# The last group of a layer's opening: all eight pairs turned by transfers, each asked for one visit behind its plane copy, and 16 conditioning passes moved behind the group

## The chip, the cores and the metric

The kernel runs on one core of one Trainium2 chip, as one program. The metric is the device time of one execution in microseconds (us); less is better. Engines are named as in the profile: PE is TensorE (PEld its weight loads), DVE is VectorE, ACT is ScalarE, POOL is GpSimd, SP is SyncE. SP computes nothing here: it holds the queue that issues nearly all transfers, in the order in which they are written.

## The reference

One conditioned decoder layer over 256 tokens of width 2048, in float32:

```python
mod = (c_act @ w_ada[l] + b_ada[l]).reshape(b, N_MOD, D_MODEL)
h = modulate(rms_norm(x, norm_ffn1[l]), mod[:, 0], mod[:, 1])
x = x + 0.5 * mod[:, 2][:, None, :] * swiglu(h, w_ffn1_gu[l], w_ffn1_down[l])
h = modulate(rms_norm(x, norm_mix[l]), mod[:, 3], mod[:, 4])
x = x + mod[:, 5][:, None, :] * token_mixing(h, w_in[l], ...)
...
def swiglu(h, w_gu, w_down):
    gate, up = jnp.split(h @ w_gu, 2, axis=-1)
    return (jax.nn.silu(gate) * up) @ w_down
```

What matters here is the first `swiglu` (the gate and up products have 5632 columns each) and the nine conditioning vectors `mod`, each a product of one row with a 2048 x 2048 block of `w_ada`.

## The kernel before

**Products.** A weight of 512 columns arrives in tiles of 128 x 4 x 512 floats (1 MB, pool `raws` with four buffers, line 106). Two of its four blocks at a time are split into a high and a low part: ACT casts the high part (`wh`, line 375), DVE subtracts it (`wl`, line 377). Pool `wsp` (line 107) holds three such pairs, so ACT can cast at most three pairs ahead of PE. For each pair PE runs 12 matmuls of 128x512 (`products`, line 354): high by high, low by high, high by low, over two halves of the tokens.

**The opening.** Because the normed input becomes ready only slowly, the first 16 chunks (8 pairs of a gate chunk and an up chunk) are not computed one after the other over the whole depth, but in four groups of blocks of the depth: blocks 0-1, 2-5, 6-11 and 12-15. Each group goes over all 16 chunks in `visit` (line 1193). The last group, `final`, has four blocks, so a visit loads one tile of 1 MB and has two pairs of weights, 24 matmuls. At the end of each turn of the loop (line 1245) `ready` asks for the tile of the next visit and casts its first pair; then `turn_step` (line 326) lets every transfer in hand do one step. After each odd visit a pair of chunks is complete and `swiglu_up` (line 695) forms silu(gate) x up for two halves of the tokens.

**Turning the result.** The product that follows needs that result transposed, in one of two ways. By PE: four transposes of 128x128 into PSUM and one eviction for each half (`transpose_to`, lines 518 and 519). By transfer (`turn_by_dma`, line 525), in three steps for each half: `apart`, two ACT copies that separate the 16-bit planes (line 535, tile `flat`); `turn`, a transposing transfer that SP issues (line 540) from `flat` into a tile `back`; `together`, two ACT copies from `back` into place (line 551). ACT's plane copies are told to stand behind the last cast issued so far. The pool `back` has four buffers (line 112): a fifth `turn` takes the buffer of the first, and so waits until the first one's `together` has read it. Before the change, pairs 0 to 5 of the group are turned by transfers and pairs 6 and 7 by PE. The steps are spread over the visits by a generator, `later` (line 651).

**Conditioning.** DVE works through `w_ada` in passes of 128x512 (line 220), four to a tile of 1 MB, which SP loads at line 215. `tick` (line 318), called after each pair of weights, does as many passes as `pace["rate"]` says. In the last group of the opening it does one pass for each pair during the first eight visits (16 passes, four tiles, taken from the pool `raws`); behind the opening, in `ffn_up` and in the product that follows, the rest, (192 - 64) / 117 to a pair. The passes of this block are due before the next norm, after that product.

**What sets the order.** Only SP's order is written by hand (line 103): its transfers stand exactly as the code issues them, and each waits for its own buffers before the next is looked at. The order on the other engines is set when the program is built, within the constraints named above; it is then fixed.

Of the kernel before, what the change touches and what calls it, by code (L numbers as in the profile page):

```python
# [77 lines left out]
def layer_kernel(  # L78
# [42 lines left out]
    def nm(s):  # L121
        uid[0] += 1
        return f"{s}_{uid[0]}"
# [10 lines left out]
    def t512():  # L134
        return tmp.tile([P, CH], F32, tag="t512", name=nm("t"))
# [173 lines left out]
    pace = {"steps": iter(()), "rate": 0.0, "due": 0.0, "behind": None}  # L309
# [14 lines left out]
    turns = []  # L324
# [189 lines left out]
    def transpose_to(dest, src_of, n, ps=None):  # L514

        ps = ps or bank()
        for j in range(n):
            nc.tensor.transpose(ps[:, j * P : (j + 1) * P], src_of(j), ident)
        nc.any.tensor_copy(dest, ps[:, : n * P])
# [5 lines left out]
    def turn_by_dma(dest, src, pool=flat, tag="flat"):  # L525


        held = {}

        def apart():  # L530
            planes = pool.tile([P, CH], F32, tag=tag, name=nm("flat"))
            planes = planes.bitcast(U16).rearrange("p (i n) -> p i n", i=2)
            with tc.issue_after(cast[-1]):
                for i in range(2):
                    nc.scalar.copy(planes[:, i, :], words(src)[:, :, i])  # L535
            held["planes"] = planes

        def turn():
            turned = back.tile([P, 2, KB, P], U16, tag="back", name=nm("back"))
            nc.sync.dma_start_transpose(  # L540
                turned.rearrange("p i k n -> p (i k) n"),
                held["planes"].rearrange("p i n -> p (i n)"),
            )
            held["turned"] = turned

        into = dest.bitcast(U16).rearrange("p k (s i) -> p k s i", i=2)

        def together():
            with tc.issue_after(cast[-1]):
                for i in range(2):  # L550
                    nc.scalar.copy(into[:, :, :, i], held["turned"][:, i])  # L551

        return apart, turn, together
# [97 lines left out]
    def later(work, then=None, quick=False):  # L651

        (a0, t0, m0), (a1, t1, m1) = work
        order = [a0, a1, None, None, None, t0, t1, None, m0]
        for f in order[:7] + order[7 + quick :]:
            yield
            if f is not None:
                f()
        m1()
        if then is not None:  # L660
            then()

    def later_by_pairs(work):

        for apart, _, _ in work:
            apart()
        for _ in range(5):
            yield
        for a in range(0, len(work), 2):
            for which in (1, 2):  # L670
                yield
                for parts in work[a : a + 2]:
                    parts[which]()
# [21 lines left out]
    def swiglu_up(banks_g, banks_u, tiles, ci, parts=None, by_dma=False, behind=None):  # L695

        k0 = ci * KB
        dest = tiles[k0 // KD].rearrange("p (k s) -> p k s", s=S)
        kk = k0 % KD
        work = []  # L700
        for t in range(NT):
            s = t512()
            g, u = banks_g[t], banks_u[t]
            if parts is not None:
                nc.vector.tensor_add(s, g, parts[0][t])
                nc.vector.tensor_add(parts[1][t], u, parts[1][t])
                g, u = s, parts[1][t]
            with nullcontext() if behind is None else tc.issue_after(behind):
                nc.scalar.activation(s, g, AF.Silu)
            nc.vector.tensor_mul(s, s, u)  # L710
            if by_dma:
                work.append(turn_by_dma(dest[:, kk : kk + KB, t * P : (t + 1) * P], s))
                continue
            transpose_to(
                dest[:, kk : kk + KB, t * P : (t + 1) * P],
                lambda j: s[:, j * P : (j + 1) * P],
                KB,
            )
        if work:
            turns.append(later(work))  # L720

    def ffn_up(held, w, tiles, first, bg=None, turned=(), ahead=None):
        for ci in range(first, DFF // CH):
# [244 lines left out]
    behind = [[back.tile([P, CH], F32, tag="back", name=nm("back")) for _ in range(NT)] for _ in range(2)]  # L968
# [181 lines left out]
    groups = [range(a, b) for a, b in zip(bounds, bounds[1:])]  # L1150
# [12 lines left out]
    def begin(n, ks):  # L1163
        raw_of = [(load_blocks(n, part), part) for part in (ks[:KB], ks[KB:]) if part]
        pieces = [
            (raw[:, a : a + 2, :], part[a : a + 2])
            for raw, part in raw_of
            for a in range(0, len(part), 2)
        ]
        prepared[n] = [  # L1170
            (lambda raw=raw, part=part: split(wsp, "w", raw[:, : len(part), :], CH), part)
            for raw, part in pieces
        ]
# [19 lines left out]
    def visit(n, ks, ends, ticks=False, ends_all=False):  # L1193
        if n not in prepared:
            begin(n, ks)
        if n not in banks:
            open_banks(n, not ends_all)
        for make, part in prepared.pop(n):
            a, b = part[0] - ks[0], part[-1] + 1 - ks[0]
            hl = slice(part[0], part[-1] + 1)  # L1200
            wh, wl = make()
            products(
                banks[n],
                held.hi[:, hl, :],
                held.lo[:, hl, :],
                wh,
                wl,
                n in fresh and a == 0,
                b == len(ks) and ends,
                seeded=n in unlinted,  # L1210
            )
            if ticks:
                tick()
        fresh.discard(n)
# [18 lines left out]
    for g, ks in enumerate(groups):  # L1233
        alone.append(g == len(groups) - 2)
        del alone[:-1]
        final = g == len(groups) - 1
        if g == len(groups) - 2:
            set_pace(ROWS_FFN1, 192, place_early, 0)
        if final:
            pace["rate"], pace["ahead"] = 1.0, 1  # L1240
        order = chunks if (len(groups) - g) % 2 else chunks[::-1]
        coming = iter(()) if final else group(groups[g + 1], 1 if g == 0 else 2)
        due = 0 if final else 2 * len(groups[g + 1])
        stay = () if final else order[-2:]
        for i, n in enumerate(order):
            if g == 0 and n in firsts:
                continue
            visit(n, ks, n not in stay, g == len(groups) - 2 or final and i < 8, final or (g == len(groups) - 2 and n in stay))
            if g:
                after = [(m, ks) for m in order[i + 1 : i + 2]]  # L1250
                if not after and not final:
                    after = [(n, groups[g + 1])]
                for m, ms in after:
                    ready(m, ms)
                    if m not in banks and not final:
                        open_banks(m, not (g == len(groups) - 2 and m in stay))
            if final:
                turn_step()
            last = len(order) - 2
            if g == 0:  # L1260
                by = [min(due, -(-j * due // 12)) for j in (i - 2, i - 1)]
                by = by[1] - by[0]
            else:
                by = (i + 1) * due // last - i * due // last if i < last else i == last
            for _ in range(by + (g == 0 and i == last)):
                next(coming, None)
            if g == 0:
                for m in {2: firsts[:1], 3: (order[2], firsts[1])}.get(i, order[i - 1 : i]):
                    if m not in stay:
                        to_parts(m)  # L1270
                if i == 3:
                    columns_rest()
                if i == 5:
                    roots_in_rows()
            if n in stay or g == 0:
                continue
            if not final:
                to_parts(n)
            elif n % 2:
                swiglu_up(  # L1280
                    banks.pop(n - 1),
                    banks.pop(n),
                    tiles,
                    n // 2,
                    (part_of(n - 1), part_of(n)),
                    n // 2 < 6,
                    cast[-1],
                )
    gate = gate_row()
    tiles.append(slot())  # L1290
    row_ring.append(two_rows())
    pace["rate"] = (192 - 64) / 117
    pace["ahead"] = AQ
    ffn_up(held, gu, tiles, EARLY, turned=range(EARLY, DFF // CH))
    gate_in = gate_load(gate, 2)
# [33 lines left out]
    work = []  # L1329
# [153 lines left out]
    for ci in range(4):  # L1483
        b = in_chunk(O_SQ + ci * CH)
        work = []
# [16 lines left out]
    for a, off in ((0, O_RQ), (1, O_RK)):  # L1502
        for ci in range(2):
            b = in_chunk(off + ci * CH)
            work = []
# [93 lines left out]
    for ci in range(4):  # L1599
        b = in_chunk(O_RG + ci * CH)  # L1600
        work = []
# [11 lines left out]
    for p in range(2):  # L1613
# [8 lines left out]
        work = []  # L1622
# [146 lines left out]
```

## Time and profile before

| | us |
|---|---|
| median of 3 runs | 2367.28 (2357.96 to 2367.73) |
| the profiled execution | 2357.64 |
| its span in the profile | 2355.5 |
| PE busy in it | 2335.7 (99%) |
| DVE busy | 1673.1 (71%) |
| ACT busy | 1367.2 (58%) |
| HBM over the span | 256 GB/s |

The profile's page gives the busy time of each engine and the chain of work that ended last, followed back from the last instruction. Other views give the busy time in chosen stretches, the instructions of one engine in order of time, the waits, and for a transfer the time from its issue to its landing. In a row of the timeline the first number is the start in us from the span's start, the second the length; `SPq` is SP's queue; `<-` in square brackets names what ended an idle time.

### The profile page before, as it was taken

Reading aid. Unit: us, or ns where it says so; the run is one execution under the profiler, and the core shown is the slowest. Engines: PE = TensorE matmul, PEld = TensorE weight load, DVE = VectorE, ACT = ScalarE, POOL = GpSimd, SP = SyncE. Lnnn points to the kernel's source line nnn. Section 1 sums busy time; section 2 is a strip of 40 time slices with the busy share of each in tenths; the row PEclk is TensorE's granted clock in tenths of the full one; section 3 lists DMA queues with packets and bytes.
Section 4 is the critical chain, followed back from the end, with each engine's and each line's share of the span. In section 5 each row is a group of like instructions: output and inputs, shape, how many; then the busy total and the mean of one; then the engine's idle time right before and its main releaser. Section 6 shows DMA issues by size and latency. Waiting matters only on the chain.

```text
span 2355.5 us, 28357 instructions
## 1 busy us (share of the span) xinstructions
PE 2335.7 (99%) x10445; PEld 1918.6 (81%) x10445; DVE 1673.1 (71%) x2576; ACT 1367.2 (58%) x1888; POOL 18.3 (1%) x27
## 2 busy tenths in 40 slices
PE   8999999999999999999999999999999999999998
PEld 5888888888888888778888888888888888888887
DVE  7788888778867768976777776676555555555656
ACT  6766567455556567774556564465455454455544
POOL 0000000000000000000000000000000000000000
PEclk9999999999999999999999999999999999999999
DMA  9989889988765889876778787754767768666553
GB/s 383 375 323 361 355 294 328 336 306 293 302 237 220 293 267 255 258 212 254 267 273 306 288 310 281 272 204 179 259 237 256 242 239 268 223 231 202 193 197 125
DMA packets 191901, 630.24 MB, mean 268 GB/s; under 512 B 113105, under 2 KB 114769, under 8 KB 121233
## 3 DMA queue, kind: packets, MB, share of 16 engines
q1 hardware_dynamic: 189266, 617.41, 74.6%
q0 software_dynamic: 1600, 9.83, 1.0%
q8 instruction: 82, 1.34, 0.2%
q10 hardware_dynamic: 896, 1.19, 0.1%
q14 instruction: 57, 0.47, 0.1%
HBM read 598.47 MB, written 4.22 MB: 256 GB/s over the span
## 4 chain that ended last, share of the span: by engine, by line
PE 96%; DMA 2%; DVE 1%; ACT 1%; issue 0%; SPq 0%; DVEq 0%; ACTq 0%
PE pa L360 93%; DMA raw<-in_w_ffn_gu_dram 1%; DMA rows_x<-in_w_ada_dram 1%; PE ps L1453 0%; DVE slot L220 0%; PE pd L1369 0%; DVE wl L377 0%; ACT wh L375 0%; DMA x_sb<-in_x_dram 0%; PE ps L360 0%; PE pa L1099 0%; PE ps L895 0%; PE pd L1099 0%; DVE rows_x L220 0%; PE ps L1369 0%
## 5 line engine op out<-in xcount | busy, mean ns | idle before, releaser
L377 DVE TENSOR_TENSOR wl<-raw,wh 128x1024 fp32r<-128x1024 f32 x792 | 963.5, 1225 | 511.0 <-ACT wh L375 451.6
L375 ACT CAST wh<-raw 128x1024 fp32r<-128x1024 f32 x792 | 830.6, 1054 | 818.7 <-PE pa L360 752.6
L360 PE MATMUL pa<-wh,hh 128*128 128x512 f32 x2184 | 597.0, 391 | 3.0 <-ACT wh L375 1.7
L360 PE MATMUL pa<-wh,hl 128*128 128x512 f32 x2184 | 592.6, 389 | 0.0
L360 PE MATMUL pa<-wl,hh 128*128 128x512 f32 x2184 | 586.2, 390 | 0.2
L360 PEld LDWEIGHTS pa<-wh,hh 128*128 128x128 f32 x2184 | 407.5, 188 | 91.6 <-ACT wh L375 2.9
L360 PEld LDWEIGHTS pa<-wl,hh 128*128 128x128 f32 x2184 | 409.4, 188 | 86.7 <-DVE wl L377 1.0
L360 PEld LDWEIGHTS pa<-wh,hl 128*128 128x128 f32 x2184 | 409.8, 188 | 86.1 <-issue 0.4
L360 PE MATMUL pa<-wh,a 128*128 128x512 f32 x1824 | 452.1, 389 | 0.0
L360 PEld LDWEIGHTS pa<-wh,a 128*128 128x128 f32 x1824 | 341.7, 188 | 70.6
L360 PE MATMUL pa<-wl,a 128*128 128x512 f32 x912 | 245.1, 389 | 0.0
L220 DVE CUSTOM_DVE_ANT_0 slot<-slot,cact 128x512 f32<-128x512 f32 (+2 forms) x288 | 219.3, 812 | 30.0 <-DMA slot<-in_w_ada_dram 29.5
L360 PEld LDWEIGHTS pa<-wl,a 128*128 128x128 f32 x912 | 171.1, 188 | 35.4
L551 ACT COPY slot<-back 128x512 uint16<-128x512 uint16 x148 | 98.7, 766 | 0.0
L220 DVE CUSTOM_DVE_ANT_0 rows_x<-rows_x,cact 128x512 f32<-128x512 f32 x124 | 78.7, 686 | 18.0 <-DMA rows_x<-in_w_ada_dram 17.8
L410 ACT CAST a<-slot 128x512 fp32r<-128x512 f32 x114 | 70.6, 620 | 29.3 <-PE pa L360 29.0
L535 ACT COPY flat<-t 128x512 uint16<-128x512 uint16 x136 | 76.7, 617 | 8.9 <-DVE t L1526 5.7
L411 DVE TENSOR_TENSOR a<-slot,a 128x512 fp32r<-128x512 f32 x114 | 77.8, 684 | 0.3 <-ACT a L410 0.3
L220 DVE CUSTOM_DVE_ANT_0 raw<-raw,cact 128x512 f32<-128x512 f32 (+1 forms) x92 | 60.7, 709 | 14.6 <-DMA raw<-in_w_ada_dram 14.5
L1219 ACT COPY slot<-pa 128x512 f32<-128x512 f32 x72 | 38.6, 589 | 21.2 <-PE pa L360 21.0
L360 PE MATMUL pa<-wh,home 128*128 128x512 f32 x160 | 39.5, 389 | 0.0
L220 DVE DVE_READ_ACCUMULATOR2_ANT sums<- 128x1 f32 x440 | 35.9, 82 | 0.0
(232 smaller groups left out, 1087.0 us busy)
## 6 DMA issues: line engine op xcount, KB each, us to landing
raw<-in_w_ffn_gu_dram SPq DMA_DIRECT2D x160, 1024.0 KB, 5.5
raw<-in_w_in_dram SPq DMA_DIRECT2D x104, 1024.0 KB, 5.8
raw<-in_w_ffn_down_dram SPq DMA_DIRECT2D x88, 1024.0 KB, 4.9
slot<-in_w_ada_dram SPq DMA_DIRECT2D x87, 1024.0 KB, 7.4
rows_x<-in_w_ada_dram SPq DMA_DIRECT2D x31, 1024.0 KB, 7.1
raw<-in_w_ada_dram SPq DMA_DIRECT2D x22, 1024.0 KB, 5.7
raw<-in_w_swa_branch_dram SPq DMA_DIRECT2D x16, 1024.0 KB, 5.0
raw<-in_w_ret_branch_dram SPq DMA_DIRECT2D x16, 1024.0 KB, 5.4
```

Of the source, the lines that this page charges most:

```text
L220: nc.vector.tensor_tensor_reduce(out=w[:, at], in0=w[:, at], in1=cact[:, at], scale=1.0, scalar=0.0, op0=ALU.mult, op1=ALU.add, accum_out= ...
L360: product = nc.tensor.matmul(banks[t], act[:, j, t * P : (t + 1) * P], weights[:, j, :], start=starts and i == 0 and j == 0, stop=ends and ...
L375: cast.append(nc.scalar.copy(hi, src).ins)
L377: low.append(nc.vector.tensor_sub(lo, src, hi.bitcast(F32)).ins)
L410: nc.scalar.copy(hi, v)
L411: nc.vector.tensor_sub(lo, v, hi.bitcast(F32))
L535: nc.scalar.copy(planes[:, i, :], words(src)[:, :, i])
L551: nc.scalar.copy(into[:, :, :, i], held["turned"][:, i])
L1219: nc.scalar.copy(p, b)
```

## The change

The last group turns all eight pairs by transfers. A new generator, `evenly`, replaces `later` there: of the two halves of a pair, the plane copy of half 0 is made in one turn, its transfer asked for in the next turn, together with the plane copy of half 1, and the transfer of half 1 in the turn after that; `together` follows four turns behind each transfer. In `later` the transfers stood four turns or more behind the plane copies, and both `together` steps in one turn. The 16 conditioning passes of the group's first eight visits are taken out; the rate behind the opening rises from (192 - 64) / 117 to (192 - 48) / 117. The rate that the group sets goes as well, since nothing ticks in it any more.

```diff
@@ -660,6 +660,14 @@
+    def evenly(work):
+
+        (a0, t0, m0), (a1, t1, m1) = work
+        for fs in ((), (a0,), (t0, a1), (t1,), (), (), (m0,), (m1,)):
+            for f in fs:
+                f()
+            yield
+
@@ -717,7 +725,7 @@
         if work:
-            turns.append(later(work))
+            turns.append((later if behind is None else evenly)(work))
@@ -1237,7 +1245,7 @@
         if final:
-            pace["rate"], pace["ahead"] = 1.0, 1
+            pace["ahead"] = 1
@@ -1245,7 +1253,7 @@
-            visit(n, ks, n not in stay, g == len(groups) - 2 or final and i < 8, final or (g == len(groups) - 2 and n in stay))
+            visit(n, ks, n not in stay, g == len(groups) - 2, final or (g == len(groups) - 2 and n in stay))
@@ -1283,13 +1291,13 @@
                     (part_of(n - 1), part_of(n)),
-                    n // 2 < 6,
+                    True,
                     cast[-1],
...
-    pace["rate"] = (192 - 64) / 117
+    pace["rate"] = (192 - 48) / 117
```

How it moves the instructions shows on three engines. First SP, in the last group. Before, the transposing transfer of `back_527` is the first that takes over a used buffer, that of `back_487` (the order is 487, 496, 507, 516, 527); the tiles are `raw_513` for visit 12, `raw_524` for visit 13, `raw_533` for visit 14:

```order
L540 DMA_TRANSPOSE back_507_2846<-flat_456_2604 128x8x128
L1158 DMA raw_513_2881<-in_w_ffn1_gu_dram 128x2048
L540 DMA_TRANSPOSE back_516_2891<-flat_466_2655 128x8x128
L1158 DMA raw_524_2936<-in_w_ffn1_gu_dram 128x2048
L540 DMA_TRANSPOSE back_527_2942<-flat_477_2705 128x8x128
L1158 DMA raw_533_2977<-in_w_ffn1_gu_dram 128x2048
```

After, the first that takes over a used buffer is `back_484`, that of `back_444` (444, 453, 464, 473, 484); `raw_481` is the tile of visit 9, `raw_490` that of visit 10:

```order
L540 DMA_TRANSPOSE back_473_2678<-flat_465_2639 128x8x128
L1166 DMA raw_481_2723<-in_w_ffn1_gu_dram 128x2048
L540 DMA_TRANSPOSE back_484_2731<-flat_474_2680 128x8x128
L1166 DMA raw_490_2766<-in_w_ffn1_gu_dram 128x2048
L540 DMA_TRANSPOSE back_493_2774<-flat_485_2733 128x8x128
L1166 DMA raw_501_2819<-in_w_ffn1_gu_dram 128x2048
```

In both, each such transfer stands between two weight tiles; after the change there is one from the tile of visit 5 on, where before they began behind that of visit 9.

Second, ACT at the same places: the `together` copies that free those buffers. Before, they stand two pairs of copies at a time, behind the cast of visit 12:

```order
L375 CAST wh_514_2883<-raw_513_2881 128x1024
L551 COPY slot_8_117<-back_487_2754 128x4x128 x2
L551 COPY slot_8_117<-back_496_2795 128x4x128 x2
L709 ACTIVATE t_518_2896<-t_518_2896 128x512
L709 ACTIVATE t_519_2901<-t_519_2901 128x512
```

After, they stand one pair to a visit, that of `back_444` behind the first cast of visit 9 and that of `back_453` behind the first cast of visit 10:

```order
L375 CAST wh_482_2725<-raw_481_2723 128x1024
L551 COPY slot_8_117<-back_444_2545 128x4x128 x2
L535 COPY flat_485_2733<-t_456_2596 128x512 x2
L375 CAST wh_488_2750<-raw_481_2723 128x1024
L375 CAST wh_491_2768<-raw_490_2766 128x1024
L551 COPY slot_8_117<-back_453_2586 128x4x128 x2
```

So before, the buffer that lets visit 14's tile be asked for is freed behind a cast of visit 12; after, the buffer that lets visit 10's tile be asked for is freed behind a cast of visit 9.

Third, PE at visit 15 of the last group. Before, the transposes of pairs 6 and 7 stand among its matmuls; the first four of them:

```order
L360 MATMUL pa_551_3055<-wh_547_3046,hh_3_112 128x512 x2
L360 MATMUL pa_551_3055<-wh_547_3046,hl_4_113 128x512
L360 MATMUL pa_552_3056<-wh_547_3046,hh_3_112 128x512 x2
L360 MATMUL pa_552_3056<-wh_547_3046,hl_4_113 128x512
L518 MATMUL ps_539_2997<-small_c_93,t_538_2992 128x128 x4
```

They stand behind the first six matmuls of the visit; after the change the 16 transposes of this stretch are gone from PE, and the 24 matmuls of a visit follow one another.

From the norm behind the first `swiglu` on, the instructions stand on every engine as before.

## The prediction

> **What bounds the kernel now.** I read the page first, then the busy times of three stretches around the last group, the chain of waits there, SP's queue and ACT in order of time, and the landing times of single transfers. The page:
>
> ```profile
> span 2355.5 us, 28357 instructions
> PE 2335.7 (99%) x10445; PEld 1918.6 (81%) x10445; DVE 1673.1 (71%) x2576; ACT 1367.2 (58%) x1888; POOL 18.3 (1%) x27
> PE 96%; DMA 2%; DVE 1%; ACT 1%; issue 0%; SPq 0%; DVEq 0%; ACTq 0%
> ```
>
> PE bounds the whole. The stretches, with the columns us, PE, PEld, DVE, ACT, POOL, granted clock, DMA share and GB/s:
>
> ```profile
> 289.00:340.00 51.00, 51.00 (x227) 42.10 (x227) 48.80 (x85) 32.97 (x43) 2.16 (x4) 1.00 0.93 330
> 340.00:385.00 45.00, 45.00 (x205) 37.26 (x204) 35.61 (x50) 38.18 (x56) 0.00 (x0) 1.00 0.86 257
> 385.00:445.00 60.00, 60.00 (x271) 49.83 (x270) 45.55 (x80) 32.56 (x40) 0.00 (x0) 1.00 0.99 360
> ```
>
> PE has no gap from before the group until behind it. So there is no idle time to win there: the change can gain only PE work that it takes out, and can lose whatever it makes PE wait. The chain of waits places the visits:
>
> ```profile
> 327.17 44.93 PE pa L360 x198
> 372.10 0.44 PE ps L518 x4
> 372.53 0.92 PE pa L360 x4
> ...
> 385.02 0.87 PE ps L518 x8
> 385.90 355.20 PE pa L360 x1567
> ```
>
> A matmul takes 355.20 / 1567 = 0.2267 us of the chain, so a visit of 24 takes 5.44 us. The transposes at 372.10 stand six matmuls into visit 15, which so began at 370.7, and visit 0 fifteen visits earlier, at 289.0 (a stray transpose there counts 0.1).
>
> **Removed from PE.** 16 transposes, 0.44 us for four: 1.8 us, all on the chain. The four evictions behind them leave ACT, which isn't on it.
>
> **Moved.** 16 passes and four tiles of 1 MB leave the first eight visits and are spread over 117 pairs of weights, some 117 x 2.72 = 318 us.
>
> ```profile
> L220 DVE CUSTOM_DVE_ANT_0 slot<-slot,cact 128x512 f32<-128x512 f32 x172 | 108.8, 686 | 17.8 <-DMA slot<-in_w_ada_dram 17.3
> 620.00:680.00 60.00, 60.00 (x267) 49.69 (x266) 51.04 (x85) 32.29 (x42) 0.00 (x0) 1.00 0.75 281
> ```
>
> 16 passes of 0.69 us are 11 us of DVE in 318, and DVE has 9 us idle in the fullest 60 quoted here (620 to 680): hidden, cost 0. The four tiles add 13 GB/s; the stretch from 385 moves 360 GB/s at a share of 0.99, the later one 281 at 0.75. If no gap of theirs were free, each would cost the 2.9 us that 1 MB takes at 360 GB/s, 12 us in all; I take 0, since PE shows no wait even in the fuller stretch. The vector whose gate goes to memory ends 13 pairs of weights later; its use lies behind the next product, so 0.
>
> **Added.** Four transposing transfers and 16 ACT copies for the halves of pairs 6 and 7. What they cost isn't their length but the queue that they stand in. SP in the last group:
>
> ```profile
> 338.20 0.33 SPq L1158 DMA_DIRECT2D raw<-in_w_ffn_gu_dram  x1
> 350.48 1.23 SPq L540 DMA_TRANSPOSE back<-flat  x1
> 351.81 0.53 SPq L1158 DMA_DIRECT2D raw<-in_w_ffn_gu_dram  x1
> 352.43 1.23 SPq L540 DMA_TRANSPOSE back<-flat  x1
> 353.76 0.74 SPq L1158 DMA_DIRECT2D raw<-in_w_ffn_gu_dram  x1
> ...
> 371.80 0.52 SPq L351 DMA_DIRECT2D raw<-in_w_ffn_gu_dram  x1
> ```
>
> From the view of SP's own waits there (us in all, times, longest):
>
> ```profile
> SPq L540 <- ACT slot L551: 34.0, 4, 13.1
> ```
>
> From 338.5 SP issues nothing for 12 us: the transfer at 350.48 waits for a used `back` buffer, and the weight tile behind it waits with it. The tile then follows 1.33 us after the transfer's start. What freed the buffer, on ACT:
>
> ```profile
> 348.10 1.06 ACT L375 CAST wh<-raw 128x1024 fp32r<-128x1024 f32 x1 [1.14 <-PE pa L360]
> 349.06 2.66 ACT L551 COPY slot<-back 128x512 uint16<-128x512 uint16 x4
> 351.58 1.15 ACT L709 ACTIVATE t<-t 128x512 f32<-128x512 f32 x2
> 352.62 1.04 ACT L375 CAST wh<-raw 128x1024 fp32r<-128x1024 f32 x1
> 353.62 1.14 ACT L535 COPY flat<-t 128x512 uint16<-128x512 uint16 x2
> 354.67 1.04 ACT L375 CAST wh<-raw 128x1024 fp32r<-128x1024 f32 x1
> ...
> 377.79 2.21 ACT L375 CAST wh<-raw 128x1024 fp32r<-128x1024 f32 x2 [0.67 <-DMA raw<-in_w_ffn_gu_dram]
> ```
>
> The copies start 0.96 us after the cast; four take 2.66, the last of them about 0.77, so two end 1.40 after their start, at 350.46, and SP's transfer starts at 350.48. That is the release, to 0.02 us. Now the landings of weight tiles behind such a transfer, and of all tiles of the stretch (minimum, median, maximum):
>
> ```profile
> L1158 SPq DMA_DIRECT2D raw<-in_w_ffn_gu_dram x1: 529/529/529, 351.8 to 351.8; - x1
> DMA to landing us min/median/max: 5.6/5.6/5.6
> L351 SPq DMA_DIRECT2D raw<-in_w_ffn_gu_dram x1: 523/523/523, 371.8 to 371.8; - x1
> DMA to landing us min/median/max: 5.9/5.9/5.9
> L1158 SPq DMA_DIRECT2D raw<-in_w_ffn_gu_dram x11: 328/333/743, 299.1 to 353.8; - x11
> DMA to landing us min/median/max: 5.2/6.5/9.2
> ```
>
> The tile issued at 371.80 landed at 377.7, and its cast began at 377.79, 0.1 later. Hence one turn of this loop, from a cast to the cast that it releases: 0.96 + 1.40 (copies) + 0.02 + 1.33 (transfer) + 5.6 (landing) + 0.1 = 9.4 us. In before the loop spans two visits, 10.9 us: the cast of visit 12 frees the buffer for the transfer ahead of visit 14's tile. It fits, and no PE wait shows. ACT's own work would fit after the change too: four casts, four copies of each kind and two silus in two visits, 4 x 0.96 + 2 x 1.05 + 2 x 1.26 + 1.04 = 9.5 of 10.9 us. But a transfer then goes out at every visit, each buffer is held for four visits, and there are four: the cast of visit 9 frees the buffer for the transfer ahead of visit 10's tile. The loop spans one visit, 5.44 us, and doesn't fit. Queued behind each waiting transfer are all later weight tiles; PE waits for them.
>
> **The sum.** ACT casts three pairs ahead, so visit 9's first cast comes when PE lets go of the high part of visit 7's second pair: four matmuls (0.9 us) before visit 8 begins at 289.0 + 8 x 5.44 = 332.5, so at 331.6. The tiles up to visit 9 go out behind plane copies of two visits earlier, two visits to a turn: no loss. Then:
> - Visits 10 to 15: six turns of 9.4, so visit 15's first cast stands at 388.0.
> - The first tile behind the group waits for copies behind visit 15's second cast. On ACT: cast 0.96, two copies 1.26, two plane copies 1.05, cast 0.96, two copies 1.40, then 0.02 + 1.33 + 5.6 + 0.1: 12.7. Cast at 400.7.
> - Four more tiles behind the group, their copies behind both casts of a tile: 9.4 + 0.96 = 10.3 each. The fifth tile's cast starts at 442.1 and ends at 443.1; then PE runs it. Behind it no transfer waits any more.
>
> Without a wait PE would begin that fifth tile at 289.0 + 20 x 5.44 = 397.8. Loss 45.3, less 1.8 for the transposes: 43.5 us. On the profiled execution's own time, 2357.64 (2.1 more than its span): 2401.1. The runs shown lie 0.3 to 10.1 above that execution, their median 9.6; I take half of that as the likely shift and forecast 2406.
>
> Unknown: the landing. With only one tile in flight it could be the 5.2 of the stretch's minimum; with the transfers' own packets and conditioning tiles beside it, its median 6.5. I take 5.6, the row with the same two transfers in the same order. Eleven turns: -4.4 to +9.9 us.
>
> A rule to weigh here: the Trainium skill, "DMA: Bandwidth & Descriptors", section "Anatomy of one DMA", fits a transfer as about 2.0 us plus its bytes at 436 GB/s (for the software path), by which 1 MB would land after 4.4 us and the loss would be an estimated 13 us less. The rows say 5.2 at least, and the measurement decides.
>
> **Rivals.**
> *The tiles are ahead anyway* (the other side). Four `raws` buffers stand ahead, and if the transfers were freed early enough the tiles would already lie there; only the transposes' 1.8 us remain: 2355.8, with the shift 2361. It decides if a turn stays under 5.44 us, so if a landing took under 1.7. For it: the group no longer lends buffers to conditioning. Against it: none of 11 tiles landed under 5.2, and SP's 12 us of silence at 338.5.
> *Only the group loses.* If the five tiles behind it were not held, because their copies come sooner than I read, PE would end visit 15 near 395.0 instead of 376.1: 19 less 1.8, 2375, with the shift 2380. Against it: SP shows the same wait behind the group already (the cast at 377.79 waits 0.67 us for its tile).
> *PE itself slows.* PE would wait 2 to 6 us at a time, some 16 times.
>
> ```profile
> 48.50:52.00 3.50, 3.41 (x15) 2.83 (x16) 3.50 (x4) 0.61 (x3) 0.00 (x0) 1.00 1.02 394
> 53.49 1.20 PE L360 MATMUL pa<-wh,hh 128*128 128x512 f32 x4 [0.97 <-ACT wh L375]
> ```
>
> Here the clock stays at 1.00 through a gap of 0.97; no longer one is quoted. If matmuls took twice as long after each wait, a visit would take 10.9 instead of a turn's 9.4, 1.5 more for six turns and 0.6 for four, and some 2 at the end: 2414, with the shift 2419. The Trainium skill, "TensorE: Matmul & The Clock Gate", section "Part 1: The HAM clock gate", says that the clock halves after an idle window of about 3.4 us; no run here shows that yet.
>
> **How the numbers follow.** Forecast 0.78, tiles ahead 0.08, only the group 0.08, slower PE 0.06. The low end, 2385, lies under the forecast's shortest landing without the shift (2396.7) by a turn or so, should one or two turns be covered; the high end, 2421, is 2401.1 + 9.9 + 10.1 and holds the slower PE. Left out: tiles ahead and only the group. 0.5% (12 us, about what a measurement of this kernel can tell from no change) is passed by all cases but the tiles ahead; only the group's lower half comes near it. Slower 0.91, same 0.07, faster 0.02: nothing in the profile could give 12 us.
>
> **What would show it.** Right: between 340 and 445 SP's queue shows pairs of transfer and tile 9 to 10 us apart, its wait for L551 copies grows from 4 times to 12 or so, PE waits in sum 40 to 50 us for casts and these for tiles, and the chain there runs through L551, the transfers and `raw`; PE is solid again from 450. Wrong: PE solid through the stretch; pairs 5.4 us apart; landings under 2 us; or waits further on, where conditioning is denser.

## The result, and the profile after

| | before | after |
|---|---|---|
| median of 4 runs, us | 2363.14 (2357.96 to 2367.73) | 2399.45 (2398.91 to 2399.67) |
| the profiled execution, us | 2357.64 | 2398.91 |
| its span, us | 2355.5 | 2396.8 |
| ratio of the times, 95% interval | | 1.0159 [1.0134, 1.0183] |

The change makes the kernel slower, by 41.3 us between the two profiled executions. The runs of before fall into two groups, near 2358 and near 2367, so their median moves with the mix; those of after lie within 0.8 us.

The page of after: the span, the busy times, PE's share and the granted clock in 40 slices of 59.9 us, the gigabytes per second, and the chain by engine.

```profile
span 2396.8 us, 28345 instructions
PE 2349.1 (98%) x10429; PEld 1924.5 (80%) x10429; DVE 1674.1 (70%) x2576; ACT 1372.9 (57%) x1900; POOL 18.9 (1%) x27
...
PE   8999997999999999999999999999999999999998
...
PEclk9999998999999999999999999999999999999999
...
GB/s 385 367 332 343 351 154 189 354 334 320 331 283 244 215 309 260 239 223 264 243 252 314 310 286 282 303 197 208 219 247 241 265 239 242 242 236 202 180 206 123
...
PE 94%; DMA 2%; ACT 2%; DVE 1%; issue 0%; SPq 0%; DVEq 0%; ACTq 0%
```

PE does 16 operations fewer than before (the transposes) and is busy 13 us longer, and still its share falls. The seventh slice, 359 to 419 us, stands out in PE and clock, and the sixth and seventh move the least data of the first half: the tiles are not late because the memory is full.

The stretch by windows (us, PE, PEld, DVE, ACT, POOL, granted clock, DMA share, GB/s), and what PE waited for in it:

```profile
289.00:331.00 42.00, 42.00 (x187) 34.79 (x186) 30.44 (x36) 26.52 (x35) 0.00 (x0) 1.00 0.59 182
331.00:441.00 110.00, 81.77 (x297) 62.29 (x297) 58.13 (x88) 57.21 (x84) 0.64 (x2) 0.88 0.60 189
441.00:501.00 60.00, 60.00 (x259) 49.52 (x258) 42.84 (x75) 30.66 (x37) 1.52 (x3) 0.97 1.03 386
...
PE pa L360 <- ACT wh L375: 28.2, 12, 4.9
```

PE is solid to 331 and again from 441. Between them 297 matmuls took 110 us; at 0.2267 each they take 67.3. Of the 42.7 us lost there, 28.2 are waits for casts and 14.4 are matmuls that ran slower (81.77 less 67.3).

SP's queue in order of time, and its waits in the stretch:

```profile
333.00 1.24 SPq L540 DMA_TRANSPOSE back<-flat  x1
334.33 0.53 SPq L1166 DMA_DIRECT2D raw<-in_w_ffn_gu_dram  x1
341.93 1.23 SPq L540 DMA_TRANSPOSE back<-flat  x1
343.25 0.53 SPq L1166 DMA_DIRECT2D raw<-in_w_ffn_gu_dram  x1
350.94 1.23 SPq L540 DMA_TRANSPOSE back<-flat  x1
352.27 0.53 SPq L1166 DMA_DIRECT2D raw<-in_w_ffn_gu_dram  x1
...
SPq L540 <- ACT flat L535: 94.6, 13, 10.2
```

Transfer and tile go out in pairs, about 9 us apart. The view of the waits says that SP waited 13 times for the plane copies of L535. ACT in order of time says otherwise:

```profile
330.62 1.05 ACT L375 CAST wh<-raw 128x1024 fp32r<-128x1024 f32 x1 [1.39 <-PE pa L360]
331.57 1.40 ACT L551 COPY slot<-back 128x512 uint16<-128x512 uint16 x2
332.84 1.13 ACT L535 COPY flat<-t 128x512 uint16<-128x512 uint16 x2
...
339.55 1.05 ACT L375 CAST wh<-raw 128x1024 fp32r<-128x1024 f32 x1 [4.63 <-DMA raw<-in_w_ffn_gu_dram]
340.50 1.40 ACT L551 COPY slot<-back 128x512 uint16<-128x512 uint16 x2
341.77 1.13 ACT L535 COPY flat<-t 128x512 uint16<-128x512 uint16 x2
```

The `together` copies begun at 331.57 and 340.50 end at 332.97 and 341.90, and the transfers start at 333.00 and 341.93: 0.03 behind the end of L551 both times, while L535 was merely running. A releaser in such a view is inferred; the ends of the candidates decide. And the cast of 339.55 waited 4.63 us for the tile issued at 334.33: the loop closes.

### The profile page after: what moved, and what is told of

It is laid out like the page before. It is cut to its first block, busy times and chain, and to the rows that moved or that the text cites. A ratio compares the mean times of both kernels' runs of the same rounds, so it can differ in the third digit from the quotient of the medians.

```text
span 2396.8 us, 28345 instructions
## 1 busy us (share of the span) xinstructions
PE 2349.1 (98%) x10429; PEld 1924.5 (80%) x10429; DVE 1674.1 (70%) x2576; ACT 1372.9 (57%) x1900; POOL 18.9 (1%) x27
## 4 chain that ended last, share of the span: by engine, by line
PE 94%; DMA 2%; ACT 2%; DVE 1%; issue 0%; SPq 0%; DVEq 0%; ACTq 0%
PE pa L360 91%; DMA raw<-in_w_ffn_gu_dram 2%; ACT wh L375 1%; DVE slot L220 1%; ACT slot L551 1%; PE ps L1461 0%; DMA slot<-in_w_ada_dram 0%; PE pd L1377 0%; ACT flat L535 0%; DMA x_sb<-in_x_dram 0%; DVE wl L377 0%; PE ps L360 0%; PE ps L903 0%; PE pd L1559 0%; PE ps L1377 0%
## 5 line engine op out<-in xcount | busy, mean ns | idle before, releaser
L220 DVE CUSTOM_DVE_ANT_0 slot<-slot,cact 128x512 f32<-128x512 f32 (+2 forms) x308 | 231.7, 803 | 8.3 <-DMA slot<-in_w_ada_dram 8.2
L551 ACT COPY slot<-back 128x512 uint16<-128x512 uint16 x156 | 105.1, 766 | 0.0
L410 ACT CAST a<-slot 128x512 fp32r<-128x512 f32 x114 | 70.5, 620 | 32.4 <-PE pa L360 29.0
L535 ACT COPY flat<-t 128x512 uint16<-128x512 uint16 x144 | 81.1, 616 | 10.2 <-DVE t L1534 5.5
L220 DVE CUSTOM_DVE_ANT_0 raw<-raw,cact 128x512 f32<-128x512 f32 (+1 forms) x72 | 47.9, 716 | 15.5 <-DMA raw<-in_w_ada_dram 15.5
```

The lines of the kernel that those rows point to most:

```text
L220: nc.vector.tensor_tensor_reduce(out=w[:, at], in0=w[:, at], in1=cact[:, at], scale=1.0, scalar=0.0, op0=ALU.mult, op1=ALU.add, accum_out= ...
L410: nc.scalar.copy(hi, v)
```

## The experiments

The theory on record: a `back` buffer is held too long, the weight tile queued behind the transfer that waits for it comes late, and the loop cast, copies, transfer, tile, cast (9 to 10 us) spans one visit (5.44 us). Rival A: the transfers stand too close behind their plane copies (what the view of SP's waits names). Rival B: the moved conditioning passes. Rival C: PE is slow by itself. Ratios are to the kernel before on the same chip, whose medians were 2356.8 us for the first four experiments below, 2357.29 for the change without `evenly` and for the last one, and 2357.35 for the other four.

**Buffers held one visit less.**

```diff
-        for fs in ((), (a0,), (t0, a1), (t1,), (), (), (m0,), (m1,)):
+        for fs in ((), (a0,), (t0, a1), (t1,), (), (m0,), (m1,)):
```

> The changed kernel, but each `together` comes one visit sooner (three turns behind its transfer instead of four), so a `back` buffer is held for three visits and the loop from cast to cast spans two visits, 10.9 us, instead of one, 5.44. Theory (buffers held too long for a loop of 9 us): PE's waits between 330 and 445 us go from about 28 us to under 5, and the time is 2356 to 2362 on a chip where before takes 2358 to 2368. Rival A (the transfers stand too close behind their plane copies, and SP waits for L535, as the view of its waits names it): nothing about that distance changes, so the waits for L535 stay and the time is 2395 to 2402. Rival B (the moved conditioning passes cost it): 2395 to 2402. Rival C (PE is slow by itself in this stretch, through its clock): 2390 or more.

2359.66 us, ratio 1.0011 [1.0001, 1.002]. PE's waits between 280 and 460 in this kernel:

```profile
PE pa L360 <- ACT wh L375: 3.2, 1, 3.2
```

One wait is left of twelve. A, B and C fall as causes of the loss, since the distance from plane copy to transfer, the passes and the matmuls stand as in the change.

**Plane copies one visit sooner, buffers held as long as in the change.**

```diff
-        for fs in ((), (a0,), (t0, a1), (t1,), (), (), (m0,), (m1,)):
+        for fs in ((a0,), (a1,), (t0,), (t1,), (), (), (m0,), (m1,)):
```

> The changed kernel, but each plane copy comes one visit (half 0) sooner, so that the transfer of half 0 stands two visits behind its plane copy instead of one; transfers and `together` copies keep their places and the buffers are held as long as in the change. Theory (held buffers): unchanged, 2396 to 2402, with turns of 9 to 10 us between the pairs of transfer and tile. Rival A (transfers too close behind the plane copies of L535): most of the loss goes, 2356 to 2370. Rival B (conditioning): unchanged, 2396 to 2402.

2399.58 us, ratio 1.0178 [1.0163, 1.0193]: the whole loss stays. SP's queue and waits in it:

```profile
334.71 1.23 SPq L540 DMA_TRANSPOSE back<-flat  x1
...
344.22 1.23 SPq L540 DMA_TRANSPOSE back<-flat  x1
...
353.43 1.23 SPq L540 DMA_TRANSPOSE back<-flat  x1
...
SPq L540 <- ACT flat L535: 81.3, 10, 9.0
```

The turns are 9.5 and 9.2 us. The view still blames L535, ten times (and L551 four times), though the plane copy that each transfer reads now lies a visit further back: rival A was an artefact of the inference.

**Conditioning back in the group.**

```diff
-            pace["ahead"] = 1
+            pace["rate"], pace["ahead"] = 1.0, 1
-            visit(n, ks, n not in stay, g == len(groups) - 2, final or (g == len(groups) - 2 and n in stay))
+            visit(n, ks, n not in stay, g == len(groups) - 2 or final and i < 8, final or (g == len(groups) - 2 and n in stay))
-    pace["rate"] = (192 - 48) / 117
+    pace["rate"] = (192 - 64) / 117
```

> The changed kernel with the 16 conditioning passes and their four tiles put back into the first eight visits of the group, at the old rates; all eight pairs are still turned by transfers one visit behind their plane copies. Theory (held buffers): 2394 to 2408, the loss stays, perhaps some us more since four more tiles stand in SP's queue. Rival B (the move of conditioning costs it): 2356 to 2368. Rival A (plane copies): 2394 to 2408.

2400.2 us, ratio 1.018 [1.0163, 1.0197]. The loss stays without the move: rival B falls a second time.

**The weight tile ahead of the waiting transfer.** In the group a tile is asked for a turn earlier; the code of all other steps is that of the change.

```diff
-        begin(n, ks)
+        if n not in prepared:
+            begin(n, ks)
...
+                for m in order[i + 2 : i + 3]:
+                    begin(m, ks)
```

> The changed kernel, but in the last group each weight tile is asked for one turn earlier, ahead of the transfer that in the change stands ahead of it; transfers, plane copies, `together` copies and buffers stay as they are. Theory (the loss comes only from weight tiles queued behind a waiting transfer on SP): a tile no longer waits for a copy behind the cast of the visit just before it, but for one behind the cast two visits before; the loop spans two visits, PE's waits in the group go from about 28 us to under 6, and the time is 2356 to 2364. If instead the late transfers cost by themselves (their results come late to the next product, or `back` is too small whatever stands behind it): 2380 or more. Rival C (PE slow by itself): 2390 or more.

2375.02 us, ratio 1.0077 [1.0062, 1.0092]: 18.2 us stay, which no theory had expected. The windows, and ACT's casts behind the group:

```profile
300.00:370.00 70.00, 70.00 (x310) 57.96 (x309) 54.38 (x66) 54.73 (x79) 0.00 (x0) 1.00 0.70 190
370.00:420.00 50.00, 36.52 (x127) 27.88 (x126) 26.14 (x52) 21.70 (x31) 0.00 (x0) 0.85 0.74 248
```

```profile
376.38 2.00 ACT L375 CAST wh<-raw 128x1024 fp32r<-128x1024 f32 x2 [4.27 <-DMA raw<-in_w_ffn_gu_dram]
...
386.30 1.99 ACT L375 CAST wh<-raw 128x1024 fp32r<-128x1024 f32 x2 [5.12 <-DMA raw<-in_w_ffn_gu_dram]
...
417.07 2.00 ACT L375 CAST wh<-raw 128x1024 fp32r<-128x1024 f32 x2 [6.84 <-DMA raw<-in_w_ffn_gu_dram]
```

The group itself is solid. Behind it, where `ffn_up` asks for the tiles and the edit does not reach, the transfer still stands ahead of each, and the first turn is 9.9 us and the four together 40.7. The expectation had forgotten that second place. So the queue order is the link in the loop: where the tile goes first, the loss is gone; where it doesn't, it stays.

**Conditioning moved, nothing else** (from the kernel before).

```diff
-            pace["rate"], pace["ahead"] = 1.0, 1
+            pace["ahead"] = 1
-            visit(n, ks, n not in stay, g == len(groups) - 2 or final and i < 8, final or (g == len(groups) - 2 and n in stay))
+            visit(n, ks, n not in stay, g == len(groups) - 2, final or (g == len(groups) - 2 and n in stay))
-    pace["rate"] = (192 - 64) / 117
+    pace["rate"] = (192 - 48) / 117
```

> The kernel before with one part of the change alone: the 16 conditioning passes leave the group's first eight visits and follow behind it at the higher rate. Pairs 6 and 7 are still turned by PE, the steps still spread as in `later`. Theory (held buffers): DVE and the transfers have room for them, ratio to before 0.998 to 1.002, no wait of PE in the group. Rival B (the denser conditioning costs): up to 12 us if no gap of the transfers were free, so a ratio of 1.003 to 1.005, or 1.018 if it were the whole loss.

2357.7 us, ratio 1.0003 [0.9994, 1.0011]: the move alone costs nothing that can be measured.

**All eight pairs by transfers, nothing else** (from the kernel before).

```diff
-                    n // 2 < 6,
+                    True,
```

> The kernel before with another part alone: all eight pairs are turned by transfers, with the steps spread as before (`later`: transfers four turns and more behind their plane copies); conditioning stays in the group. Theory: both `together` copies of a pair come in one turn, so each buffer wait spans two visits; the 16 transposes go (1.8 us), and a few us may come back where the last tiles stand behind the late transfers of pairs 6 and 7: ratio 0.999 to 1.004. Rival D (four more transfers and 16 more copies cost by themselves, whatever the spacing): 1.012 to 1.018.

2356.24 us, ratio 0.9993 [0.9977, 1.0008], with a single wait of PE in the stretch, 0.6 us. With the old spacing, four more transfers and 16 more copies cost nothing that can be measured.

**The change without `evenly`.**

```diff
-            turns.append((later if behind is None else evenly)(work))
+            turns.append(later(work))
```

> The changed kernel without `evenly`: all eight pairs by transfers and the passes moved, but the steps spread as in `later`, as before the change. Theory (held buffers): each of these two parts alone cost nothing, and both together cost at most the 3 us of the wait behind the group: ratio 0.998 to 1.002. If the two parts together were what makes the loop, and the spacing of `evenly` not: 1.012 to 1.018.

2357.19 us, ratio 1.0003 [0.9994, 1.0012]; PE waits three times in the stretch, 1.5 us in all. The two parts together cost nothing that can be measured either. The loss comes with the spacing of `evenly`.

**Five buffers, the order in the code untouched.** `back` gets five buffers; `flat` gives up one of three to make room.

```diff
-    flat = ctx.enter_context(tc.tile_pool(name="flat", bufs=3))
-    back = ctx.enter_context(tc.tile_pool(name="back", bufs=4))
+    flat = ctx.enter_context(tc.tile_pool(name="flat", bufs=2))
+    back = ctx.enter_context(tc.tile_pool(name="back", bufs=5))
```

> The changed kernel with the order of all steps untouched, but five buffers in `back` instead of four; to make room for it, `flat` has two instead of three. Theory (held buffers): a transfer waits for the copies of the fifth one back instead of the fourth, a visit earlier, so the loop spans two visits and the loss goes but for a few us behind the group: ratio 1.000 to 1.005, unless two `flat` buffers cost something elsewhere in the kernel, which the trace would show behind 470 us. Rival A (transfers too close behind the plane copies) and rival B (conditioning): 1.016 to 1.020.

2360.54 us, ratio 1.0013 [1.0005, 1.0022]. The windows:

```profile
330.00:380.00 50.00, 50.00 (x222) 41.44 (x221) 37.36 (x47) 41.97 (x62) 0.00 (x0) 1.00 0.84 234
380.00:390.00 10.00, 6.92 (x23) 5.21 (x23) 9.36 (x21) 7.06 (x10) 0.00 (x0) 0.83 1.01 364
390.00:440.00 50.00, 50.00 (x222) 41.23 (x221) 38.90 (x73) 29.99 (x39) 2.17 (x4) 1.00 1.02 398
```

SP's queue keeps the order of the change. On ACT, whose order is set anew when the program is built, the second cast of L410 moves behind the casts of the first tile behind the group, and some of DVE's operations move too; the group's copies and casts on ACT keep their order. One more buffer takes the loop away, although `flat` has one less: the held buffer is shown, and it and the holding time can be exchanged. One wait stays near 384, much as with `together` a visit sooner.

**`together` two visits sooner.**

```diff
-        for fs in ((), (a0,), (t0, a1), (t1,), (), (), (m0,), (m1,)):
+        for fs in ((), (a0,), (t0, a1), (t1,), (m0,), (m1,)):
```

> The changed kernel with each `together` two visits sooner (two turns behind its transfer). With one visit sooner nearly all of the loss went; what stayed was one wait of PE, 3.2 us, at the second tile behind the group. Theory (held buffers): a buffer is then held for two visits, the loop spans three, 16.3 us against turns of 9 to 10.3, also behind the group, where copies stand behind the second cast of a tile: no wait is left, and the 16 transposes are won, ratio 0.998 to 1.000. If the wait of 3.2 us had another cause (the end of the group itself, conditioning tiles in the queue): 1.000 to 1.002 as with one visit sooner. If the copies now come too close behind the transfers, ACT waits for their landing: 1.002 or more.

2360.51 us, ratio 1.0013 [1.0004, 1.0021]: no better than one visit sooner, with the same wait (3.3 us). So this remainder isn't the held buffer; the theory's form of this run missed. What stands ahead of it, in the kernel with `together` one visit sooner, DVE first, then ACT:

```profile
378.23 0.68 DVE L220 CUSTOM_DVE_ANT_0 slot<-slot,cact 128x512 f32<-128x512 f32 x1
...
380.68 1.29 DVE L718 TENSOR_TENSOR t<-t,a 128x512 f32<-128x512 f32 x2
```

```profile
382.00 0.62 ACT L410 CAST a<-slot 128x512 fp32r<-128x512 f32 x1 [4.03 <-DVE t L718]
382.67 2.00 ACT L375 CAST wh<-raw 128x1024 fp32r<-128x1024 f32 x2
```

Four conditioning passes, 378.23 to 380.68, stand on DVE ahead of L718; ACT's cast L410 waits for L718; the weight cast stands behind it on ACT.

**`together` one visit sooner, and conditioning back in the group** (the edits of the first and third experiment in one kernel).

> The changed kernel with each `together` one visit sooner and the 16 conditioning passes back in the group's first eight visits. With `together` sooner and the passes moved, one wait of PE of 3.2 us stayed behind the group, where four conditioning passes stand on DVE ahead of L718, and the next weight cast stands on ACT behind a cast (L410) that waits for it. Theory: the held buffers made the loop, and this remainder is the moved passes at that place; with both undone the wait falls under 1 us and the 16 transposes are won: ratio 0.998 to 1.000, PE busy 2333 to 2336 of a span of about 2353 to 2355. If the remainder has another cause (the late transfers of pairs 6 and 7): the wait stays, ratio 1.001 to 1.002. If the four conditioning tiles in SP's queue of the group disturb a loop of two visits: 1.003 or more.

2362.36 us, ratio 1.0017 [1.0006, 1.0028]: missed. The wait of 3.2 us is gone, but PE now waits four times, three of them behind the group:

```profile
347.90 1.20 PE L360 MATMUL pa<-wh,hh 128*128 128x512 f32 x4 [1.27 <-ACT wh L375]
...
379.56 1.20 PE L360 MATMUL pa<-wh,hh 128*128 128x512 f32 x4 [1.16 <-ACT wh L375]
...
385.90 1.20 PE L360 MATMUL pa<-wh,hh 128*128 128x512 f32 x4 [0.61 <-ACT wh L375]
...
398.77 1.19 PE L360 MATMUL pa<-wh,hh 128*128 128x512 f32 x4 [1.49 <-ACT wh L375]
```

The casts ahead of the last two, on ACT:

```profile
384.80 2.00 ACT L375 CAST wh<-raw 128x1024 fp32r<-128x1024 f32 x2 [2.04 <-DMA raw<-in_w_ffn_gu_dram]
...
397.68 2.00 ACT L375 CAST wh<-raw 128x1024 fp32r<-128x1024 f32 x2 [3.85 <-DMA raw<-in_w_ffn_gu_dram]
```

These two casts waited for tiles that landed 7.9 and 7.1 us after their issue. The run doesn't test the passes by themselves: four of them still stand ahead of L718 (383.01 to 385.46), but here ACT's cast of 384.80 stands ahead of L410 and needn't wait for it. So how much the passes ahead of L718 cost is not shown; they are at most a part of the remainder. In the forms of `evenly` without the loop 3 to 5 us stay; in the runs with `later` none can be measured. Where these us come from stays open. No version tried is measurably faster than before.

## Why the prediction was right, and where it was off

**The mechanism and its place** are shown from both sides: holding each buffer for a visit less, a fifth buffer, or the old spacing each take the loop away; moving plane copies or passes does not. The sign named for it, some 12 waits of SP for L551 copies, showed under the name L535; the starts of the transfers, 0.03 us behind the ends of L551, say that it is the same wait.

**The sum, term by term.** In the profiled execution 443.1 was forecast for the fifth tile behind the group on PE; it came at 438.56.
- Visit 9's first cast: 331.6 forecast, 330.62 measured, 1.0 earlier: the visits began that much sooner.
- Six turns: 56.4 forecast (6 x 9.4). The last of the seven casts (the first, 330.62, stands above), and the first and the fifth behind the group, on ACT:

```profile
384.99 1.05 ACT L375 CAST wh<-raw 128x1024 fp32r<-128x1024 f32 x1 [3.83 <-DMA raw<-in_w_ffn_gu_dram]
...
397.22 1.99 ACT L375 CAST wh<-raw 128x1024 fp32r<-128x1024 f32 x2 [0.24 <-DMA raw<-in_w_ffn_gu_dram]
...
437.46 1.99 ACT L375 CAST wh<-raw 128x1024 fp32r<-128x1024 f32 x2 [2.75 <-DMA raw<-in_w_ffn_gu_dram]
```

384.99 less 330.62 is 54.4: 9.06 a turn, 2.0 less in all.
- The first tile behind the group: 12.7 forecast, 397.22 less 384.99 = 12.2.
- Four more: 41.4 forecast (4 x 10.36, there written 10.3), 437.46 less 397.22 = 40.2.
- The fifth tile's cast until PE runs it: 1.0 forecast, 438.56 less 437.46 = 1.1.

Together 4.5 us less than forecast, 1.0 of it from the earlier start and the rest from the turns. The mis-sized term of the turns is the landing: 5.6 was taken from the one row with the same two transfers; the tiles of the group, issued at L1166, show 5.1 to 5.4 (minimum, median, maximum):

```profile
DMA to landing us min/median/max: 5.1/5.2/5.4
```

With one tile in flight the value lay at the forecast's low end, which the text had named as possible. The estimate of 4.4 us from the fit of the Trainium skill ("DMA: Bandwidth & Descriptors", section "Anatomy of one DMA") lies below each of these landings. That fit is for the software path; 618 of the 631 MB here go through a queue that the profile calls hardware_dynamic, so no landing here tests the fit on its own path.

**The clock.** The rival "PE itself slows" was given 0.06 and a price of 13 us. That matmuls slow down is real; that they do so after each wait, and the price, were wrong. PE from the fifth tile on, in the chain of after:

```profile
438.56 344.44 PE pa L360 x1506
```

1506 matmuls at 0.2267 take 341.4; the 3.0 us above that are the slow ones right behind the last gap. The slow matmuls before that (14.4 us in the stretch to 441, of which about 1.2 belong to those 3.0) ran while the next tile was still on its way, so they only shortened PE's waits. In one place the chain goes through them, 23 matmuls in 7.12 us:

```profile
367.98 7.12 PE pa L360 x23
```

There a cast waited for DVE behind these matmuls instead of for its tile, and the turn stayed at 8.9 us. That is also why PE's waits came to 28.2 and not to the 40 to 50 named as a sign. So 43.5 - 4.5 + 3.0 = 42.0 against the 41.9 by which after reaches the end of this piece of the chain later (783.00 against before's 741.10), and 41.3 at the end of the program. That the forecast of 43.5 came so close is in part luck: its two errors, the turns that were shorter and the slow matmuls that the sum left out, have opposite signs.

**Costed at nothing, and nothing:** the move of the passes, 1.0003 [0.9994, 1.0011] alone. The 1.8 us of the transposes do not show apart: all eight pairs by transfers alone give 0.9993 [0.9977, 1.0008], which holds both that gain and none.

**The shift of the runs.** Half of the 9.6 us by which before's shown median lay above its profiled execution was added. After's median lies 0.5 above its own. That step was wrong: after did not inherit the offset. The two misses of size, 2.2 us (43.5 for 41.3) and this 4.3, make the difference from 2406 to 2399.45.

**The other rivals.** "Tiles ahead anyway" needed a landing under 1.7 us; of the tiles in this stretch none was under 5.1. "Only the group loses" is the reverse of the run with the tile first, in which only the five tiles behind it were late, and that alone cost 18.2 us.

## What to carry to other kernels

SP's queue is issued in order, so a transfer that waits for a buffer delays every load behind it: with the tile asked for ahead of the transfer, the group had no wait left. Where such loads feed the work that frees the buffer, compare the loop's time with the visits that it spans (buffers less visits held, plus one: in the change 4 - 4 + 1). Here 9 us in two visits of 5.44 cost nothing before the change, in one visit it cost 41 us, and one more buffer or one visit less of holding gave back all but some 3 us. Asking for a transfer sooner is not free if its buffer is let go no sooner.

## What the runs showed of the hardware

Matmuls ran slower behind some gaps of PE of less than 2 us, and not behind others. Those right behind two gaps of nearly one length, and behind the longest, in after:

```profile
386.08 1.74 PE L360 MATMUL pa<-wh,hh 128*128 128x512 f32 x4 [1.82 <-ACT wh L375]
387.62 1.91 PE L360 MATMUL pa<-wh,hl 128*128 128x512 f32 x4
...
398.32 2.07 PE L360 MATMUL pa<-wh,hh 128*128 128x512 f32 x4 [4.89 <-ACT wh L375]
400.19 1.91 PE L360 MATMUL pa<-wh,hl 128*128 128x512 f32 x4
401.90 1.87 PE L360 MATMUL pa<-wl,hh 128*128 128x512 f32 x4
403.60 1.08 PE L360 MATMUL pa<-wh,hh 128*128 128x512 f32 x4
...
428.57 1.20 PE L360 MATMUL pa<-wh,hh 128*128 128x512 f32 x4 [1.83 <-ACT wh L375]
429.60 1.07 PE L360 MATMUL pa<-wh,hl 128*128 128x512 f32 x4
```

Behind 4.89 us of idleness, groups of four start 1.70 to 1.87 us apart for 5.3 us, instead of 0.91, and the granted clock there is 0.50. Slow groups follow a gap of 1.82 at 386.08 too (granted clock 0.66 from 386 to 391), but not one of 1.83 at 428.57 (1.00 from 428.5 to 434), so the length of the gap alone doesn't decide. The Trainium skill, "TensorE: Matmul & The Clock Gate", section "Part 1: The HAM clock gate", describes a free-running window of about 3.4 us, with half the clock after an idle one and full clock after a busy one. The trace agrees with a clock of about half (1.71 for four, 428 ns each; the page has 426.7 for a cold matmul of this width) and, by the two equal gaps, is consistent with a window that runs freely; it does not agree that a whole 3.4 us of idleness is needed. What share of a window must be idle, no run here shows.
